# Column-group products of five places in a hybrid trunk issued as unbroken runs on TensorE

## The chip, the cores and the metric

One core of a Trainium2 chip runs the whole program in one launch. The metric is device time in microseconds (us), the median of three runs. The core has five engines that run side by side, each through its own list of instructions, in order: TensorE (PE in the profile; PEld is its weight load), VectorE (DVE), ScalarE (ACT), GpSimd (POOL) and SyncE (SP, which here only issues loads). They wait for each other at semaphores.

A matrix product on TensorE writes up to 128 partitions of PSUM. A *column-group product* has a stationary operand of only 32 or 64 columns and writes 32 or 64 partitions; four products of 32 columns, or two of 64, fill the width of the array.

## What is computed

Four layers over 256 latent and 256 context tokens of width 1024, each with another mixer and then a mixture of 16 experts (top 1 group of 4, top 2 experts in it). All in fp32.

```python
for i in range(DEPTH):                       # 4 layers
    mod_x = silu(c) @ w_mod[i] + b_mod[i]    # (1, 6*D); the same for the context, from c_ctx
    sh1, sc1, g1, sh2, sc2, g2 = split(mod, 6)
    h = rmsnorm(x) * (1 + sc1) + sh1
    y = [windowed_gqa, mamba2_bidir, mlstm_bidir, mla][i](h_ctx, h_lat, ...)
    x = x + g1 * y
    x = x + g2 * hier_moe(rmsnorm(x) * (1 + sc2) + sh2, ...)
return rmsnorm(x)
```

The five places of the change are the two rows `silu(c) @ w_mod`, the last product of each attention (`p @ v` in `windowed_gqa` and in `mla`), the product of `mamba2_bidir` inside a chunk (`einsum('blsg,blsge,bsgep->blgep', cb, lmat, u)`), and the chunk states of `mlstm_bidir` (`einsum('bsh,bshd,bshv->bhdv', ws, k, v)`).

## The kernel before

The program is written in Python and fully unrolled: 9,431 instructions on TensorE in the main part. A scheduler puts them in order. It walks the instructions with a priority (the order in which they are written) and with its own estimate of when operands are ready, and appends to each engine's list what is ready by that estimate; `issue_after(x)` adds "not before x on this engine", and `high_priority()` lets what is traced inside go ahead of other ready work. A product that is ready early by the estimate can thus be listed ahead of the products that belong beside it, with other work between them.

- **Modulation** (`mod_round`, product on L231). Each layer needs three rounds of 2048 columns. A round is 8 steps; a step loads a 1 MB piece of `w_mod` into a ring of four buffers `w` (`wload`, L182, on SP's queue, shared with the other weights) and makes four products, 32 columns stationary (`cs`, all steps), 512 wide, into the four quarters of one PSUM tile `wm`. 96 steps in all. Steps are put into a queue and popped by `fill` between pieces of the mixers, so they stand among the mixer's own products.
- **Values of layer 0** (`values`, L1128). For each of 4 token tiles and 4 key-value heads: transposes of the probabilities (L1118) into `tr`, ACT moves them to `PT` (L1122), then 4 or 8 products of 64 columns, 256 wide, into the two halves of a PSUM tile `core`, over `k` (2 or 4 key blocks) and `par` (even and odd heads). `probs` of the next block (scores, L1088) is written ahead of it.
- **Last product of a head pair in layer 1** (`head`, L1398): 8 products of 64 columns, 128 wide, for 16 pairs. It takes `A`, which DVE finished last.
- **mLSTM states** (`mlstm_states`, L1635): 12 times four products of 64 columns, 130 wide.
- **Values of layer 3** (`mla_core`, L1927): 8 times 8 products of 64 columns, 256 wide, over 4 key blocks and `h` (two heads).

The large plain products around them come from `mm3` (L207 to L209): a product of split fp32 as three passes.

Of the kernel before, what the change touches and what calls it, by code (L numbers as in the profile page):

```python
# [23 lines left out]
class Trunk:  # L24
# [172 lines left out]
    def split(self, pool, w, shape, name="split", bufs=3):  # L197
# [5 lines left out]
        return hi, lo  # L203

    def mm3(self, ps, a, b, start, stop):
        mm = self.nc.tensor.matmul
        mm(ps, a[0], b[0], start=start, stop=False)  # L207
        mm(ps, a[0], b[1], start=False, stop=False)  # L208
        self.last_mm = mm(ps, a[1], b[0], start=False, stop=stop)  # L209


    def mod_round(self, i, r):

        nc, I = self.nc, self.I
        st = {}

        def step(j, load=None):
# [11 lines left out]
            w = load([src]) if load else self.wload(src, [128, 2048])  # L229
            for g in range(4):  # L230
                nc.tensor.matmul(st["ps"][32 * g:32 * g + 32, :], self.cs[:, j, :], w[:, 512 * g:512 * g + 512],  # L231
                                 start=(j == 0), stop=(j == 7))

# [828 lines left out]
    def attn_core(self, pool, pout, kz, vr, qT):  # L1062
# [45 lines left out]
        def values(t, kv, pr, sm):  # L1108
# [16 lines left out]
            po = self.core()  # L1125
            for k in range(nk):
                for par in range(2):
                    nc.tensor.matmul(po[par * 64:(par + 1) * 64, :256], vr[:, k, kv * 64:(kv + 1) * 64],  # L1128
                                     PT[k // 2][:, k % 2, par::2, :], start=(k == 0), stop=(k == nk - 1))
            pv = po[:, :256].rearrange("p (m q) -> p m q", m=2)  # L1130
# [164 lines left out]
    def ssm_main(self, pool, late, mid, keep, heads):  # L1295
# [46 lines left out]
        def head(ft, zt, xs, xr, CT, Br, CB, gs, first):  # L1342
# [52 lines left out]
            py = self.core()  # L1395
            for c in range(4):
                for h in range(2):
                    nc.tensor.matmul(py[64 * h:64 * h + 64, tok(c)], xr[:, 128 * c + 64 * h:128 * c + 64 * h + 64],  # L1398
                                     M[0][:, h, c, :], start=True, stop=True)
            y = xs  # L1400
# [208 lines left out]
    def mlstm_states(self, pool, keep, kT, va, gt):  # L1609
# [16 lines left out]
        for d, order in ((0, (0, 1, 2, 3)), (1, (1, 0, 3, 2))):  # L1626
            for n in range(3):
                c, nx = order[n], order[n + 1]
                s = keep.tile([128, 4, 130], F32, name=f"cst{d}{n}")
                for ab in range(2):  # L1630
                    ps = self.core()
                    for a in (2 * ab, 2 * ab + 1):
                        for h in range(2):
                            hd = 2 * a + h
                            nc.tensor.matmul(ps[64 * h:64 * h + 64, (a % 2) * 130:(a % 2) * 130 + 130],  # L1635
                                             kw[c, d][:, hd * 64:hd * 64 + 64], va[c][:, hd, :], start=True, stop=True)
                    for a in (2 * ab, 2 * ab + 1):
                        v = ps[:, (a % 2) * 130:(a % 2) * 130 + 130]
                        if n == 0:
                            nc.scalar.activation(s[:, a, :], v, AF.Copy)  # L1640
                        else:
                            nc.vector.scalar_tensor_tensor(s[:, a, :], st[c, d][:, a, :], gt["cw"][:, d, a, c:c + 1], v,
                                                           op0=OP.mult, op1=OP.add)
                st[nx, d] = s
# [249 lines left out]
    def mla_core(self, pool, kT, vr, qT, ohi, olo):  # L1894
        nc, I = self.nc, self.I
        sc = 96.0 ** -0.5
        for a in range(8):
            po = self.core()
            PT = []
            for h in range(2):  # L1900
# [22 lines left out]
                PT.append(pt)  # L1923
            for k in range(4):
                for h in range(2):
                    hd = 2 * a + h
                    nc.tensor.matmul(po[64 * h:64 * h + 64, :256], vr[k][:, hd * 64:hd * 64 + 64],  # L1927
                                     PT[h][:, k].rearrange("p t q -> p (t q)"), start=(k == 0), stop=(k == 3))
            hh, ll = ohi[a // 2][:, a % 2, :], olo[a // 2][:, a % 2, :]
# [154 lines left out]
```

## Time and profile before

| | |
|---|---|
| runs | 2065.24 us median (2065.15 to 2068.01) |
| profiled execution | 2062.44 us, of which the span of instructions is 2060.3 us |
| TensorE busy | 1899.6 us (92%) |
| VectorE busy | 1394.9 us (68%) |
| ScalarE busy | 1036.1 us (50%) |
| GpSimd busy | 536.4 us (26%) |
| granted TensorE clock, mean | 0.963 of 2.4 GHz |
| read from memory | 452.41 MB, 234 GB/s over the span with what is written |

In the rows of a timeline, the first number is the start in us from the begin of the span, the second how long it lasted, then engine, line, operation, what it writes and reads, shape (partitions times columns of the stationary operand, then the moving operand), count. An fp32 product leaves two records in the trace, so "x8" of L231 is four products. Products are pipelined: how long one holds TensorE is read from its start to the start of the next instruction, not from its own length.

### The profile page before, as it was taken

How to read it: one execution, taken by the hardware profiler on the slowest of the kernel's cores; microseconds unless marked ns; L12 is line 12 of the kernel's file. 1: busy time of each engine (PE TensorE's matmuls, PEld its weight loads, DVE VectorE, ACT ScalarE, POOL GpSimd, SP SyncE). 2: the span in 40 equal slices, each digit the busy share in tenths (PEclk: the TensorE clock that was granted, in tenths of full speed). 3: DMA queues.
4: the chain of work that ended last, by engine and by line, in shares of the span. 5: the costliest groups of instructions: out<-in, count | busy, mean ns of one | idle time of the engine just before them, and what ended most of it. 6: DMA issues, size and time to landing. Idle time of an engine off the chain costs nothing. (4 is left out here: it accounts for less than half of the span.)

```text
span 2060.3 us, 30756 instructions
## 1 busy us (share of the span) xinstructions
PE 1899.6 (92%) x11036; PEld 1411.8 (69%) x11036; DVE 1394.9 (68%) x2728; ACT 1036.1 (50%) x2172; POOL 536.4 (26%) x525
## 2 busy tenths in 40 slices
PE   5999988999999999998799899996979999998996
PEld 2875686777767778776577678885867766656542
DVE  3568557886598787777788662338578876486444
ACT  2447526775575555433577542245457755454111
POOL 2012232213475555445221410004241132001000
PEclk8999998999999999999899999998989999999998
DMA  9344667986486546547798557542669966807792
GB/s 342 137 164 166 244 208 275 400 304 191 135 252 210 158 169 200 180 141 269 266 391 339 164 163 265 189 164 90 236 215 378 401 194 228 296 11 277 285 368 94
DMA packets 172915, 471.73 MB, mean 229 GB/s; under 512 B 27769, under 2 KB 74993, under 8 KB 152272
## 3 DMA queue, kind: packets, MB, share of 16 engines
q1 hardware_dynamic: 148912, 401.98, 54.3%
q0 software_dynamic: 23136, 65.86, 10.0%
q8 instruction: 90, 1.47, 0.3%
q10 hardware_dynamic: 704, 1.82, 0.2%
q14 instruction: 73, 0.60, 0.1%
HBM read 452.41 MB, written 29.77 MB: 234 GB/s over the span
## 5 line engine op out<-in xcount | busy, mean ns | idle before, releaser
L758 DVE TENSOR_TENSOR elo<-wl,ehi 128x1024 fp32r<-128x1024 f32 x156 | 187.0, 1220 | 27.8 <-ACT ehi L757 26.9
L757 ACT ACTIVATE ehi<-wl 128x1024 fp32r<-128x1024 f32 x156 | 161.6, 1055 | 51.8 <-PE acc L209 32.7
L231 PE MATMUL wm<-w,cs 128*32 128x512 f32 x768 | 125.2, 640 | 22.7 <-DMA w<-in_w_mod_dram 22.7
L763 POOL DMA_INDIRECT xg<-hd,gi x48 | 64.0, 1334 | 281.9 <-PE tr L776 224.0
L1292 POOL TENSOR_TENSOR wcl<-w,wch 128x512 fp32r<-128x512 f32 x76 | 114.2, 1515 | 81.8 <-ACT wch L1291 75.7
L207 PE MATMUL acc<-hhi,wch 128*128 128x512 f32 (+1 forms) x336 | 131.8, 393 | 0.5 <-ACT wch L1291 0.5
L209 PE MATMUL acc<-split_hi,hlo 128*128 128x256 f32 x464 | 131.3, 285 | 0.0
L209 PE MATMUL acc<-hhi,wcl 128*128 128x512 f32 (+1 forms) x336 | 129.8, 388 | 1.4 <-POOL wcl L1292 1.4
L208 PE MATMUL acc<-split_lo,hhi 128*128 128x256 f32 x464 | 131.0, 285 | 0.0
L207 PE MATMUL acc<-split_hi,hhi 128*128 128x256 f32 x464 | 131.0, 286 | 0.0
L208 PE MATMUL acc<-hlo,wch 128*128 128x512 f32 (+1 forms) x336 | 129.9, 387 | 0.0
L207 PE MATMUL acc<-ehi,xTh 128*128 128x512 f32 x288 | 123.6, 429 | 2.2 <-ACT xTh L779 2.2
L208 PE MATMUL acc<-elo,xTh 128*128 128x512 f32 x288 | 117.8, 409 | 1.1 <-DVE elo L758 1.1
L209 PE MATMUL acc<-ehi,xTl 128*128 128x512 f32 x288 | 115.6, 401 | 0.0
L758 DVE TENSOR_TENSOR elo<-w,ehi 128x1024 fp32r<-128x1024 f32 x84 | 100.9, 1218 | 13.6 <-ACT ehi L757 13.1
L757 ACT ACTIVATE ehi<-w 128x1024 fp32r<-128x1024 f32 x84 | 87.0, 1052 | 26.2 <-PE acc L209 14.8
L1370 ACT ACTIVATE A<-A,lnb 128x128 f32<-128x128 f32 x256 | 78.6, 388 | 39.4 <-POOL A L1365 39.4
L207 PEld LDWEIGHTS acc<-split_hi,hhi 128*128 128x128 f32 x464 | 88.1, 191 | 9.4 <-issue 3.5
L202 DVE TENSOR_TENSOR split_lo<-w,split_hi 128x1024 fp32r<-128x1024 f32 x33 | 40.1, 1224 | 80.3 <-ACT split_hi L201 80.0
L209 PEld LDWEIGHTS acc<-split_hi,hlo 128*128 128x128 f32 x464 | 88.5, 191 | 3.2 <-DVE split_lo L202 0.8
L386 POOL TENSOR_TENSOR x<-x,restmp 128x256 f32<-128x256 f32 (+1 forms) x46 | 48.2, 1047 | 160.1 <-DVE restmp L382 146.0
L208 PEld LDWEIGHTS acc<-split_lo,hhi 128*128 128x128 f32 x464 | 88.5, 191 | 0.7 <-issue 0.7
(625 smaller groups left out, 5456.9 us busy)
## 6 DMA issues: line engine op xcount, KB each, us to landing
w<-in_w_mod_dram SPq DMA_DIRECT2D x96, 1024.0 KB
wl<-in_moe_w_down_dram SPq DMA_DIRECT2D x47, 1024.0 KB
wl<-in_moe_w_gate_dram SPq DMA_DIRECT2D x82, 512.0 KB
wl<-in_moe_w_up_dram SPq DMA_DIRECT2D x82, 512.0 KB
w<-in_moe_w_gate_dram SPq DMA_DIRECT2D x46, 512.0 KB
w<-in_moe_w_up_dram SPq DMA_DIRECT2D x46, 512.0 KB
w<-in_ssm_w_in_dram SPq DMA_DIRECT2D x40, 512.0 KB
yd<-y POOLq DMA_DIRECT2D x39, 512.0 KB, 9.6
```

The lines of the kernel that those rows point to most:

```text
L202: self.nc.vector.tensor_sub(lo, w, hi)
L207: mm(ps, a[0], b[0], start=start, stop=False)
L208: mm(ps, a[0], b[1], start=False, stop=False)
L209: self.last_mm = mm(ps, a[1], b[0], start=False, stop=stop)
L231: nc.tensor.matmul(st["ps"][32 * g:32 * g + 32, :], self.cs[:, j, :], w[:, 512 * g:512 * g + 512], start=(j == 0), stop=(j == 7))
L386: (nc.vector if last else nc.gpsimd).tensor_add(x, x, tmp)
L757: nc.scalar.activation(hi, v, AF.Copy)
L758: nc.vector.tensor_sub(lo, v, hi)
L763: nc.gpsimd.indirect_dma_start(out=xgs[e % len(xgs)], out_offset=None, in_=self.hd, in_offset=bass.IndirectOffsetOnAxis(ap=self.gi[:, e:e ...
L1292: (eng or self.nc.gpsimd).tensor_sub(lo, v, hi)
L1370: nc.scalar.activation(M[d][:, h, c], M[d][:, h, c], AF.Exp, bias=self.lb[:, c, k:k + 1])
```

## The change

A helper `together` issues the products of a group so that all but the first get high priority and an edge behind the first. Five loops use it. Two of them also go in another order: in layer 0 the values start with the last key block and the odd heads, in layer 3 with the second head of the pair. No product, load or copy is added or taken away.

```diff
+    def together(self, jobs):
+
+        jobs = list(jobs)
+        first = jobs[0]()
+        with self.tc.issue_after(first.ins), self.tc.high_priority():
+            for m in jobs[1:]:
+                m()
+
...
-            for g in range(4):
-                nc.tensor.matmul(st["ps"][32 * g:32 * g + 32, :], self.cs[:, j, :], w[:, 512 * g:512 * g + 512],
-                                 start=(j == 0), stop=(j == 7))
+            self.together(lambda g=g: nc.tensor.matmul(
+                st["ps"][32 * g:32 * g + 32, :], self.cs[:, j, :], w[:, 512 * g:512 * g + 512],
+                start=(j == 0), stop=(j == 7)) for g in range(4))
...
-            for k in range(nk):
-                for par in range(2):
-                    nc.tensor.matmul(po[par * 64:(par + 1) * 64, :256], vr[:, k, kv * 64:(kv + 1) * 64],
-                                     PT[k // 2][:, k % 2, par::2, :], start=(k == 0), stop=(k == nk - 1))
+            self.together(lambda k=k, par=par: nc.tensor.matmul(
+                po[par * 64:(par + 1) * 64, :256], vr[:, k, kv * 64:(kv + 1) * 64],
+                PT[k // 2][:, k % 2, par::2, :], start=(k == nk - 1), stop=(k == 0))
+                for k in range(nk - 1, -1, -1) for par in (1, 0))
...
-            for c in range(4):
-                for h in range(2):
-                    nc.tensor.matmul(py[64 * h:64 * h + 64, tok(c)], xr[:, 128 * c + 64 * h:128 * c + 64 * h + 64],
-                                     M[0][:, h, c, :], start=True, stop=True)
+            self.together(lambda c=c, h=h: nc.tensor.matmul(
+                py[64 * h:64 * h + 64, tok(c)], xr[:, 128 * c + 64 * h:128 * c + 64 * h + 64],
+                M[0][:, h, c, :], start=True, stop=True) for c in range(4) for h in range(2))
```

The mLSTM states (order kept) and the values of layer 3 (`for k in range(4) for h in (1, 0)`) are rewritten in the same way.

What the scheduler makes of it, counted in TensorE's order. A run is an unbroken stretch of products of one place (two neighbouring steps make one run); in a run, each four products of 32 columns, or two of 64, are one started four or pair, and a rest counts as one.

| place | groups | broken before | runs before, after | fours or pairs before, after |
|---|---|---|---|---|
| modulation | 96 | 18 | 91, 74 | 115, 96 |
| values, layer 0 | 16 | 14 | 31, 16 | 62, 48 |
| last product, layer 1 | 16 | 9 | 30, 16 | 73, 64 |
| mLSTM states | 12 | 2 | 11, 11 | 26, 24 |
| values, layer 3 | 8 | 7 | 15, 8 | 39, 32 |

After the change no group is broken. The rest of the order is nearly kept: the lists hold the same instructions, and 2,690 of 9,431 on TensorE stand at another place, few of them by more than 30. Ten modulation steps begin 22 to 168 instructions earlier than before; no step's load moves by more than 4 places in SP's queue.

TensorE in layer 1, two modulation steps (`w_8217`, `w_8223`) among products of the output projection (`acc`) and of the heads' states (`core_7992`, `tr_7987`). Before; the other three products of `w_8223` stand 124 instructions further on:

```order
L1379 MATMUL core_7992<-ud_7951,Br_7399 128x128 x2
L231 MATMUL wm_7028<-w_8217,cs_78 32x512 x3
L1393 MATMUL tr_7987<-CT_7398,st0_7981 128x128
L231 MATMUL wm_7028<-w_8217,cs_78 32x512
L231 MATMUL wm_7028<-w_8223,cs_78 32x512
L207 MATMUL acc_7875<-wch_7859,yh0_7024 128x512
```

After:

```order
L1387 MATMUL core_7992<-ud_7951,Br_7399 128x128
L238 MATMUL wm_7028<-w_8217,cs_78 32x512 x4
L1401 MATMUL tr_7987<-CT_7398,st0_7981 128x128 x2
L238 MATMUL wm_7028<-w_8223,cs_78 32x512 x4
L215 MATMUL acc_7875<-wch_7859,yh0_7024 128x512
```

Both steps are whole; `w_8223` has come together at the place of its first product.

TensorE in layer 0, the value products `core_2277` of one block, with transposes `tr` of it and of the next block, and scores `acc` (each ended by a mask product on `identb`). Before:

```order
L1118 MATMUL tr_2270<-ident_85,p_2142 128x128 x4
L1128 MATMUL core_2277<-PT_2243,vr_214 64x256
L1118 MATMUL tr_2340<-ident_85,p_2210 128x128 x4
L1088 MATMUL acc_2391<-kh1_208,qT1_216 128x512
L1088 MATMUL acc_2391<-kl1_209,qT1_216 128x512
L1093 LDWEIGHTS identb_87
L1093 MATMUL acc_2391<-mj1_1354,identb_87 128x128
L1088 MATMUL acc_2400<-kh1_208,qT1_216 128x512
L1088 MATMUL acc_2400<-kl1_209,qT1_216 128x512
L1093 LDWEIGHTS identb_87
L1093 MATMUL acc_2400<-mj1_1354,identb_87 128x128
L1128 MATMUL core_2277<-PT_2243,vr_214 64x256 x3
```

After:

```order
L1126 MATMUL tr_2270<-ident_85,p_2142 128x128 x4
L1126 MATMUL tr_2340<-ident_85,p_2210 128x128 x4
L1134 MATMUL core_2277<-PT_2244,vr_214 64x256 x4
L1134 MATMUL core_2277<-PT_2243,vr_214 64x256 x4
L1126 MATMUL tr_2348<-ident_85,p_2219 128x128 x4
```

The lone product is gone, and the run begins with the operand that is made last (`PT_2244`, the second half of the key blocks); the scores that stood between the last transposes and the run stand elsewhere.

TensorE at the start of layer 3, two modulation steps (`w_17371`, `w_17377`) among the products of the latent projection (`acc_17162`, `acc_17205`). After the change they stand here:

```order
L217 MATMUL acc_17162<-lkv_hi_17152,hlo0_16944 128x288
L238 MATMUL wm_17352<-w_17371,cs_78 32x512 x4
L337 MATMUL tr_17031<-dg_17017,x1_70 128x128 x4
L337 MATMUL tr_17068<-dg_17066,x2_71 128x128 x4
L215 MATMUL acc_17162<-lkv_hi_17152,hhi1_16943 128x288
L216 MATMUL acc_17162<-lkv_lo_17153,hhi1_16943 128x288
L215 MATMUL acc_17205<-lkv_hi_17148,hhi0_16942 128x288
L216 MATMUL acc_17205<-lkv_lo_17149,hhi0_16942 128x288
L238 MATMUL wm_17352<-w_17377,cs_78 32x512 x4
```

Before, the first began 36 instructions later than here and the second 82 later, the first of them broken in two:

```order
L329 MATMUL tr_17080<-dg_17066,x2_71 128x128 x4
L231 MATMUL wm_17352<-w_17371,cs_78 32x512
L329 MATMUL tr_17116<-dg_17114,x3_72 128x128 x4
...
L208 MATMUL acc_17248<-lkv_lo_17153,hhi1_16943 128x288
L231 MATMUL wm_17352<-w_17371,cs_78 32x512 x3
L1813 MATMUL tr_17197<-ident_85,lrow_17189 128x128 x2
```

These are two of the ten steps that have moved ahead by more than 20 instructions.

## Rows read from the trace of the kernel before

**Rows 1.** The page, part 1: busy us of each engine (share), instructions.

```profile
PE 1899.6 (92%) x11036; PEld 1411.8 (69%) x11036; DVE 1394.9 (68%) x2728; ACT 1036.1 (50%) x2172; POOL 536.4 (26%) x525
```

**Rows 2.** Windows: length, then PE, PEld, DVE, ACT, POOL busy, clock, DMA, GB/s.

```profile
40.00:131.00 91.00, 90.64 (x729) 81.07 (x730) 54.63 (x126) 38.92 (x86) 0.58 (x1) 1.00 0.45 163
135.00:245.00 110.00, 106.31 (x672) 59.29 (x671) 78.34 (x253) 75.49 (x256) 30.92 (x29) 0.96 0.52 183
545.00:945.00 400.00, 392.60 (x2135) 300.39 (x2133) 314.50 (x506) 208.60 (x504) 206.79 (x153) 1.00 0.59 189
...
1705.00:1795.00 90.00, 82.08 (x525) 57.75 (x526) 49.85 (x98) 44.11 (x105) 8.39 (x14) 0.94 0.70 249
1805.00:1866.00 61.00, 60.51 (x314) 32.88 (x312) 50.14 (x146) 33.47 (x85) 0.00 (x0) 1.00 0.12 38
```

**Rows 3.** Lines by form: count, busy us, mean ns, idle us before, what ended it.

```profile
L231 PE MATMUL wm<-w,cs 128*32 128x512 f32 x768 | 125.2, 640 | 22.7 <-DMA w<-in_w_mod_dram 22.7
...
L1128 PE MATMUL core<-PT,vr 128*64 128x256 f32 x192 | 33.7, 392 | 0.5 <-ACT PT L1122 0.5
...
L1398 PE MATMUL core<-A,xr 128*64 128x128 f32 x256 | 22.9, 287 | 0.0
```

**Rows 4.** Timeline of PE in layer 0's projection: a whole and a lone L231.

```profile
42.85 1.07 PE L231 MATMUL wm<-w,cs 128*32 128x512 f32 x8
43.85 0.39 PE L209 MATMUL acc<-split_hi,hlo 128*128 128x256 f32 x1
...
50.97 0.28 PE L207 MATMUL acc<-split_hi,hhi 128*128 128x256 f32 x1
51.09 0.28 PE L208 MATMUL acc<-split_lo,hhi 128*128 128x256 f32 x1
51.30 1.04 PE L231 MATMUL wm<-w,cs 128*32 128x512 f32 x2
52.28 0.38 PE L209 MATMUL acc<-split_hi,hlo 128*128 128x256 f32 x1
52.50 0.28 PE L207 MATMUL acc<-split_hi,hhi 128*128 128x256 f32 x1
```

**Rows 5.** Timeline of PE in layer 0's attention: a broken value group.

```profile
231.10 0.66 PE L1118 MATMUL tr<-ident,p 128*128 128x128 f32 x4
231.69 0.65 PE L1128 MATMUL core<-PT,vr 128*64 128x256 f32 x2
232.27 0.66 PE L1118 MATMUL tr<-ident,p 128*128 128x128 f32 x4
232.85 1.94 PE L1128 MATMUL core<-PT,vr 128*64 128x256 f32 x14
234.72 1.09 PE L1118 MATMUL tr<-ident,p 128*128 128x128 f32 x8
```

**Rows 6.** Timeline of PE in layer 1: a whole and a broken last product.

```profile
578.42 1.09 PE L1398 MATMUL core<-A,xr 128*64 128x128 f32 x16
579.44 0.49 PE L1379 MATMUL core<-ud,Br 128*128 128x128 f32 x2
...
663.67 0.49 PE L1393 MATMUL tr<-CT,st 128*128 128x128 f32 x2
664.09 0.44 PE L1398 MATMUL core<-A,xr 128*64 128x128 f32 x4
664.46 0.71 PE L1393 MATMUL tr<-CT,st 128*128 128x128 f32 x4
```

**Rows 7.** Timeline of PE and ACT in layer 0: last transposes and their move.

```profile
236.18 0.63 PE L1118 MATMUL tr<-ident,p 128*128 128x128 f32 x4 [0.36 <-issue]
...
236.84 0.66 ACT L1122 ACTIVATE PT<-tr 128x256 f32<-128x256 f32 x2 [0.21 <-PE tr L1118]
```

**Rows 8.** Timeline of SP and PE in layer 2: a load and its products.

```profile
1437.09 0.33 SPq L182 DMA_DIRECT2D w<-in_w_mod_dram  x1
...
1442.03 1.07 PE L231 MATMUL wm<-w,cs 128*32 128x512 f32 x8 [0.81 <-DMA w<-in_w_mod_dram]
```

More of the change, by code (lines that the diff above doesn't have):

```diff
@@ L1631, in mlstm_states @@
                     ps = self.core()
[L1632 to L1636, printed above, removed]
+                    self.together(lambda a=a, h=h: nc.tensor.matmul(
+                        ps[64 * h:64 * h + 64, (a % 2) * 130:(a % 2) * 130 + 130],
+                        kw[c, d][:, (2 * a + h) * 64:(2 * a + h) * 64 + 64], va[c][:, 2 * a + h, :],
+                        start=True, stop=True) for a in (2 * ab, 2 * ab + 1) for h in range(2))
                     for a in (2 * ab, 2 * ab + 1):
@@ L1923, in mla_core @@
                 PT.append(pt)
[L1924 to L1928, printed above, removed]
+            self.together(lambda k=k, h=h: nc.tensor.matmul(
+                po[64 * h:64 * h + 64, :256], vr[k][:, (2 * a + h) * 64:(2 * a + h) * 64 + 64],
+                PT[h][:, k].rearrange("p t q -> p (t q)"), start=(k == 0), stop=(k == 3))
+                for k in range(4) for h in (1, 0))
             hh, ll = ohi[a // 2][:, a % 2, :], olo[a // 2][:, a % 2, :]
```

## Prediction

> **What bounds the kernel now.** I read the page's busy line first: TensorE is busy 92% of the span, VectorE 68%, ScalarE 50% [rows 1]. That is a mean, so the table of windows came next, for the stretches in which the five places stand [rows 2]. Compare PE with DVE in each. In layer 0's projection PE is busy 90.64 of 91 us, DVE 54.63. In layer 0's attention PE has 106.31 of 110, DVE 78.34, ACT 75.49. In layer 1's mixer PE has 392.60 of 400, DVE 314.50 (79%). At layer 3's start PE has 82.08 of 90, with the most transfers (DMA share 0.70). In layer 3's attention PE has 60.51 of 61 and DVE 50.14. So PE sets the pace in all of them, with nothing much in reserve on DVE in layer 1 and in both attentions. The groups by line say what ends PE's idle time [rows 3]: ahead of the values 0.5 us in all, ahead of layer 1's last products none, ahead of the modulation 22.7 us, all of it by the load of `w`. A us that one of these products holds PE for nothing is a us of the end, except where another engine is just behind.
>
> The timeline then gives the price of a broken group, from starts to next starts. A whole modulation step, four products, holds PE from 42.85 to 43.85, 1.00 us; a lone product of the same shape holds it from 51.30 to 52.28, 0.98 us [rows 4]. The four quarters run side by side, and a product cut off from its three neighbours pays for all of them.
>
> **The change part by part.** It neither adds nor removes an instruction; it saves fours and pairs, and the two ends of each run.
>
> *Price of a four, a pair and an end.* A product split off costs a further four. A lone four costs 0.98; I take 0.86 for one more inside a neighbouring run and 0.12 as fixed, since a usual step between plain products of this stage is 0.12 (50.97 to 51.09). The ends: 51.09 to 51.30 is 0.21 where 0.12 is usual, and 52.28 to 52.50 is 0.22 where 0.12 is usual, so 0.19 for both ends together [rows 4]. A run less thus saves 0.31 beside its fours. Values, 256 wide: a lone product takes 231.69 to 232.27, 0.58 us; seven (four pairs) take 232.85 to 234.72, 1.87 [rows 5]. The difference, 1.29 for three pairs, is 0.43 a pair, and 0.15 of the lone one is fixed; with the 0.19 a run costs 0.34. Layer 1's last products: eight take 578.42 to 579.44, 1.02, and a two-product piece 664.09 to 664.46, 0.37 [rows 6]; the difference over three pairs is 0.22 a pair, fixed again 0.15.
>
> *The sum.* Counts are those of the table under the change. Modulation: 19 fours by 0.86 and 17 runs by 0.31, 21.6 us. Values of layer 0: 14 pairs by 0.43 and 15 runs by 0.34, 11.1. Layer 1's last products: 9 by 0.22 and 14 by 0.34, 6.7. mLSTM states: 2 pairs by about 0.22 (130 wide, nearest to 128), 0.4. Values of layer 3: no row of theirs stands here; they have the shape of layer 0's, so 7 by 0.43 and 7 by 0.34, 5.4, with bounds from nothing to that. Together 45.2 us of PE's time. By stage, with the modulation's fours and runs counted in the order: layer 0 projection 2 fours and 1 run, 2.0; layer 0 attention 11.1; layer 1 mixer 11 and 10, 12.6, and 6.7, so 19.3; layer 2 mixer 3 and 3, 3.5, and 0.4, so 3.9; layer 3 start 3 and 3, 3.5; layer 3 attention 5.4.
>
> The Trainium skill (TensorE: Matmul & The Clock Gate, section "The mechanism" of Part 3) says the opposite of the row on which this rests: a weight load overlaps a running product only where the row group differs, and these four share all 128 rows and differ in columns alone. By that rule four would cost 4 times 0.98 instead of 1.00, an unbroken step would save nothing but the ends, and the kernel would stay where it is; by the row it saves as above, and the row decides.
>
> *What is late next, layer 0.* The run of values now starts with the operand that is made last (second place of the order). The last four transposes begin at 236.18 and ACT has moved them at 236.84 + 0.66 = 237.50, 1.32 us later [rows 7]. Before, scores stood between them and the rest of the values; now in places only one set of transposes does (231.10 to 231.69, 0.59 [rows 5]), and the head of the run would wait up to 0.73. Where nothing stands between, it waits about 1.3 less the transposes' own 0.6. The bounds are nothing and 1.32 for each of 16 blocks. I count 4 of 16 blocks, those at the end where no scores are left to go between, at 0.8: 3.2 lost, 7.9 left. Behind the waiting product everything on PE queues; transposes and scores of the next block then reach ACT and DVE later, but PE is what these wait for.
>
> *Layer 1.* DVE is busy 79% and the products that go into the run take `A`, its last product. I let 80% of 19.3 through, 15.4; bounds a quarter and all of it.
>
> *Layer 2* passes whole, 3.9. *Layer 3 start:* steps `w_17371` and `w_17377` have moved ahead by 36 and 82 instructions (third place of the order) while their loads stand where they stood in SP's queue. From a load's issue to its first product 4.94 us pass where PE is already waiting, and 0.81 of that was wait (1437.09 to 1442.03) [rows 8]. The bounds for a moved step are nothing (the ring holds four pieces, so a load is issued ahead) and 4.9; I let half of the 3.5 go, 1.7 left. *Layer 3 attention:* DVE 50.14 of 61 [rows 2]; 80% of 5.4, 4.3.
>
> Sum: 2.0 + 7.9 + 15.4 + 3.9 + 1.7 + 4.3 = 35.2 us. The profiled execution took 2062.4 (2060.3 span and 2.1 around it), so 2027.2; the median of the runs lies 2.8 above that execution, which gives 2030.
>
> **The rivals.** *A, forecast:* 2030, its own range 2020 (all 45.2 pass) to 2043 (half of it). *B, another engine takes over:* in layer 0's attention, layer 1 and layer 3's attention only a quarter comes through, (11.1 + 19.3 + 5.4)/4 = 9.0, with the other 7.6 makes 16.6, so 2049. For it: ACT and DVE above two thirds of layer 0's window, DVE 79 to 82% in the others. Against it: PE has next to no idle time there, so nothing else was ever the last to end [rows 2, 3].
>
> *C, the heads wait:* each of the 24 value runs (16 and 8) waits 1.32 for its last operand, 31.7; in place of the 3.2 above that leaves 6.7, so 2059. For it: the first product now takes the newest operand. Against it: the broken groups had a product right behind the newest operand too, and idled 0.5 us in all 192 [rows 3]. The same section of the Trainium skill says that products start and end strictly in order, by which a waiting head holds up all behind it; the 0.36 of idle time in [rows 7] is of that kind.
>
> *D, slower:* the ten modulation steps that begin 22 to 168 instructions earlier each wait for a whole load. Ten by 4.94 is 49.4, against 45.2 saved: 4.2 lost, 2069. It decides from a mean wait of 4.5 us. For it: a load's end is the one thing that ends idle time ahead of this line, 22.7 us already [rows 3]. Against: those are spread over 96 steps, and DMA has half its time free in layer 1 (share 0.59) [rows 2].
>
> *E, the change does nothing:* unbroken products don't run side by side after all, and a run of four costs four times 0.98: 2065. Against it stands the whole step of 1.00 us, and 78 of the 96 steps were whole already, so they give no other price than the one in [rows 4].
>
> **How the numbers follow.** A 0.64, B 0.21, C 0.06, D 0.06, E 0.03. The time is A's, 2030. The range goes from 2017, all of the 45.2 with prices 7% higher, to 2053, just above B; D, E and most of C lie outside it. A change of less than 0.2%, 4 us, can't be told from none here. Faster: A, B and half of C, 0.88. Same: the other half of C and E, 0.06. Slower: D, 0.06.
>
> **What would show it.** Of the profile after: every modulation record in the timeline comes as eight or a multiple, holding PE about 1.00 us for four (prices); the busy time of PE falls by 2 in layer 0's projection and some 19 over layer 1 (sums); the values of layer 0 show idle time ahead of them by ACT's `PT` of about 3 us, not 20 (A against C); the modulation's idle time by DMA stays near 22.7, at most a few us more (A against D); DVE's and ACT's share of the stages rises as these become shorter, with PE's idle share still small (A against B). I am wrong if PE's stages shrink but an idle share of the same size appears in them (B, C, D), or if single products of a column group turn out to be cheaper elsewhere than in the two places that I priced.

## The result and the profile after

The changed kernel takes 2029.79 us (median of 4 runs, 2027.54 to 2031.01), the kernel before 2065.19 in the same comparison (2064.59 to 2068.01): ratio 0.9829, 95% interval 0.9816 to 0.9842, or 35 us less. The forecast was 2030. The profiled execution took 2027.54, its span is 2025.7; of before these were 2062.44 and 2060.3.

The page of the changed kernel, part 1 (it answers to [rows 1]). TensorE is busy 39 us less and its weight loads (PEld) 14 less; the other engines work as long as before:

```profile
PE 1860.5 (92%) x11036; PEld 1398.2 (69%) x11036; DVE 1393.5 (69%) x2728; ACT 1035.9 (51%) x2172; POOL 535.5 (26%) x525
```

Groups by line and form, of after (answering to [rows 3]; the last is layer 3's values). The busy time of the modulation falls from 125.2 to 107.0, of layer 0's values from 33.7 to 24.3, of layer 1's last products from 22.9 to 17.5, of layer 3's values from 20.7 (first line, of before) to 15.6:

```profile
L1927 PE MATMUL core<-PT,vr 128*64 128x256 f32 x128 | 20.7, 389 | 0.2 <-ACT PT L1920 0.2
...
L238 PE MATMUL wm<-w,cs 128*32 128x512 f32 x768 | 107.0, 645 | 22.3 <-DMA w<-in_w_mod_dram 22.3
...
L1134 PE MATMUL core<-PT,vr 128*64 128x256 f32 x192 | 24.3, 388 | 1.8 <-ACT PT L1130 1.7
L1404 PE MATMUL core<-A,xr 128*64 128x128 f32 x256 | 17.5, 279 | 0.0
L1930 PE MATMUL core<-PT,vr 128*64 128x256 f32 x128 | 15.6, 385 | 0.7 <-ACT PT L1926 0.7
```

Two places in TensorE's timeline of after. The modulation step that was broken in [rows 4] has come together (51.27 to 52.26, 0.99 us, where one product alone had taken 0.98); and the value products of layer 0 come as 16 records, eight products, in 1.88 us, with a short wait for their last operand:

```profile
51.27 1.07 PE L238 MATMUL wm<-w,cs 128*32 128x512 f32 x8
52.26 0.38 PE L217 MATMUL acc<-split_hi,hlo 128*128 128x256 f32 x1
...
219.94 1.04 PE L1126 MATMUL tr<-ident,p 128*128 128x128 f32 x8
221.29 1.95 PE L1134 MATMUL core<-PT,vr 128*64 128x256 f32 x16 [0.31 <-ACT PT L1130]
223.17 1.09 PE L1126 MATMUL tr<-ident,p 128*128 128x128 f32 x8
```

Where the time came from is read from windows that begin and end with the same instructions in both kernels: layer 0's projection, layer 0's attention, layer 1's mixer, layer 1's experts with the norm behind them, layer 2's projections and states, layer 2's chunks with the output projection, layer 3's start, layer 3's attention. Columns as in [rows 2]. Of before:

```profile
40.94:129.90 88.96, 88.62 (x716) 79.05 (x714) 52.61 (x120) 37.98 (x85) 0.58 (x1) 1.00 0.44 161
129.90:245.88 115.98, 108.77 (x690) 61.12 (x686) 83.69 (x268) 78.74 (x262) 30.92 (x29) 0.96 0.52 183
506.13:965.35 459.22, 449.56 (x2461) 346.87 (x2461) 349.76 (x559) 234.11 (x548) 230.22 (x172) 0.99 0.59 191
965.35:1184.37 219.02, 195.80 (x957) 146.78 (x956) 178.25 (x300) 139.04 (x221) 59.38 (x68) 0.95 0.79 284
1184.37:1372.01 187.64, 186.64 (x1363) 154.41 (x1362) 68.05 (x138) 59.09 (x111) 11.94 (x22) 1.00 0.56 197
1372.01:1501.00 128.99, 104.56 (x759) 94.38 (x760) 93.50 (x255) 66.82 (x203) 43.34 (x43) 0.92 0.44 156
1712.15:1801.54 89.39, 82.02 (x528) 60.10 (x527) 47.38 (x90) 43.40 (x104) 9.18 (x15) 0.94 0.71 254
1801.54:1867.11 65.57, 64.02 (x323) 34.13 (x321) 52.93 (x153) 36.22 (x91) 0.86 (x2) 1.00 0.15 52
```

The same of after:

```profile
40.92:127.88 86.96, 86.62 (x715) 78.66 (x714) 52.62 (x120) 38.28 (x85) 0.58 (x1) 1.00 0.47 165
127.88:236.49 108.61, 99.31 (x691) 57.61 (x687) 83.50 (x268) 77.61 (x262) 31.02 (x29) 0.97 0.52 179
495.97:940.36 444.39, 432.74 (x2461) 342.46 (x2460) 352.11 (x562) 234.88 (x549) 225.35 (x173) 0.99 0.60 198
940.36:1162.75 222.39, 198.61 (x958) 148.94 (x956) 176.90 (x298) 138.86 (x221) 60.26 (x67) 0.93 0.78 280
1162.75:1347.89 185.14, 184.09 (x1364) 153.73 (x1362) 68.40 (x138) 59.35 (x111) 11.99 (x22) 1.00 0.57 200
1347.89:1470.52 122.63, 102.51 (x763) 92.50 (x764) 92.25 (x256) 67.05 (x203) 43.70 (x43) 0.93 0.46 164
1683.03:1770.59 87.56, 78.26 (x519) 59.42 (x518) 46.52 (x90) 42.59 (x102) 10.33 (x16) 0.92 0.71 259
1770.59:1832.48 61.89, 59.26 (x323) 33.19 (x321) 52.06 (x153) 36.20 (x91) 0.00 (x0) 1.00 0.15 53
```

Length less PE busy is TensorE's idle time. Against the forecast (left forecast, right measured, us; layer 2 is its two windows together):

| stage | PE busy less | idle more | stage shorter |
|---|---|---|---|
| layer 0 projection | 2.0, 2.0 | 0, 0 | 2.0, 2.0 |
| layer 0 attention | 11.1, 9.5 | 3.2, 2.1 | 7.9, 7.4 |
| layer 1 mixer | 19.3, 16.8 | 3.9, 2.0 | 15.4, 14.8 |
| layer 2 mixer | 3.9, 4.6 | 0, -4.3 | 3.9, 8.9 |
| layer 3 start | 3.5, 3.8 | 1.8, 1.9 | 1.7, 1.8 |
| layer 3 attention | 5.4, 4.8 | 1.1, 1.1 | 4.3, 3.7 |
| sum | 45.2, 41.5 | 10.0, 2.8 | 35.2, 38.6 |

The spans differ by 34.6, so the rest of the program became 4.0 longer, most of it layer 1's experts (219.02 to 222.39). One row of the table isn't what it seems. Of the moved modulation steps one left layer 3's start for the stretch ahead of it, so the windows of layer 3's start don't hold the same work: 112 records of the modulation before and 104 after, eight less, which is one step of four products. In these windows of L231 and L238 alone PE's busy time stands behind the length:

```profile
1712.15:1801.54 89.39, 17.62 (x112) 0.94 0.71 254
1683.03:1770.59 87.56, 13.64 (x104) 0.92 0.71 259
```

With a step at 1.0 us, layer 3's start saved 2.8 of PE's time and became 0.8 shorter, and 1.0 of the 4.0 elsewhere is that step. Four of six stages came out within 0.6 us of the forecast and layer 3's start 0.9 below it; layer 2 gave 5 us more, and the rest of the program took 3 back.

### The profile page after: what moved, and what is told of

The parts are those of the page before. It is cut to its first block, busy times and chain, and to the rows that moved or that the text cites. A ratio compares the mean times of both kernels' runs of the same rounds, so it can differ in the third digit from the quotient of the medians.

```text
span 2025.7 us, 30765 instructions
## 1 busy us (share of the span) xinstructions
PE 1860.5 (92%) x11036; PEld 1398.2 (69%) x11036; DVE 1393.5 (69%) x2728; ACT 1035.9 (51%) x2172; POOL 535.5 (26%) x525
## 5 line engine op out<-in xcount | busy, mean ns | idle before, releaser
L238 PE MATMUL wm<-w,cs 128*32 128x512 f32 x768 | 107.0, 645 | 22.3 <-DMA w<-in_w_mod_dram 22.3
```

Source lines behind the costliest of these rows:

```text
L238: self.together(lambda g=g: nc.tensor.matmul(st["ps"][32 * g:32 * g + 32, :], self.cs[:, j, :], w[:, 512 * g:512 * g + 512], start=(j == 0 ...
```

## The experiments

**Each place by itself.** Five kernels take one hunk of the change each and leave the other places as before. Of the modulation:

```diff
-            for g in range(4):
-                nc.tensor.matmul(st["ps"][32 * g:32 * g + 32, :], self.cs[:, j, :], ...
+            self.together(lambda g=g: nc.tensor.matmul(
+                st["ps"][32 * g:32 * g + 32, :], self.cs[:, j, :], ...
```

> Only the modulation steps are made unbroken. In TensorE's order their runs go from 91 to 74 and their fours from 115 to 96, as in the full change; the other four places stay broken (values of layer 0 31 runs, last products 29, values of layer 3 15). Theory (prices of fours and ends, each passed on as in the stages of the prediction): 2.0 + 12.6 by 0.8 + 3.5 + 1.7 = 17 us less than before, 2048. Rival (the gain of the full change came from the rest of the order, which the scheduler also changed): the loss per place can't be added up, and this kernel lies outside 2043 to 2053. In layer 2's last chunk the scores stand in TensorE's order as one block of 8, not in two of 4 as after the full change; if that order is what took 4 us of idle time out of layer 2's mixer, the idle time there stays near 24 us here.

Of layer 0's values:

```diff
-            for k in range(nk):
-                for par in range(2):
+            self.together(lambda k=k, par=par: ...
+                for k in range(nk - 1, -1, -1) for par in (1, 0))
```

> Only the values of layer 0 are made unbroken (31 runs to 16, 62 pairs to 48), and with them the scheduler happens to save 2 runs and 1 four of the modulation. Theory: 11.1 us of TensorE's time, of which some 2 to 3 come back as idle time in the attention; 8 to 9 less, and 1 for the modulation: about 2056. Rival (waits at the heads of the 16 runs, up to 1.3 us each): 2062 or more, with idle time ahead of the values well above the 1.8 us of the full change.

Of layer 1's last products:

```diff
-            for c in range(4):
-                for h in range(2):
+            self.together(lambda c=c, h=h: ... for c in range(4) for h in range(2))
```

> Only layer 1's last products are made unbroken (30 runs to 16, 73 pairs to 64); the modulation loses 3 runs and 1 four by the way. Theory of prices alone: 6.7 and 1.8 us by 0.8, so 7 less: 2058. In layer 2's last chunk TensorE's order is here the same as after the full change (the scores in two blocks of 4), though nothing in layer 2 was changed. If that order is what took the idle time out of layer 2's mixer, a further 4 us go there, idle time 20 us in place of 24, and the time is 2054. If the idle time went for another reason (the modulation steps or the states), it stays at 24 and the time is 2058.

Of layer 3's values:

```diff
-            for k in range(4):
-                for h in range(2):
+            self.together(lambda k=k, h=h: ... for k in range(4) for h in (1, 0))
```

> Only the values of layer 3 are made unbroken (15 runs to 8, 39 pairs to 32); all else stands as before. Theory: 5.4 us of TensorE's time less in layer 3's attention, about 1 of it back as idle time: 4 less, 2061, and no other stage changes by more than 1. Rival (DVE takes over there): 1.4 less, 2064, with the freed time as idle time ended by DVE.

Of layer 2's states:

```diff
-                    for a in (2 * ab, 2 * ab + 1):
-                        for h in range(2):
+                    self.together(lambda a=a, h=h: ... for a in (2 * ab, 2 * ab + 1) for h in range(2))
```

> Only the states of layer 2 are made unbroken (26 pairs to 24, runs 11 as before). Theory: 0.4 us, which can't be told from none: 2065 within 3 us, and the idle time of layer 2's mixer stays near 24 us. If the states were what took it out, it is 20 here and the time 2061.

| kernel | median, us | ratio to before (95%) | own stages shorter by, us | layer 2 chunks and output, us |
|---|---|---|---|---|
| modulation | 2040.55 | 0.9875 (0.9857 to 0.9893) | 2.0, 7.9, 2.4, 2.0 | 120.25 |
| values, layer 0 | 2049.80 | 0.9915 (0.9900 to 0.9929) | 6.6 | 120.70 |
| last products, layer 1 | 2058.02 | 0.9959 (0.9943 to 0.9975) | 5.4 | 122.70 |
| values, layer 3 | 2060.73 | 0.9974 (0.9964 to 0.9983) | 3.7 | 128.87 |
| states, layer 2 | 2062.89 (one run) | | | 128.82 |
| before | 2066.18 (2065.34 beside the states) | | | 128.99 |

In its own stages each place gives about what it gives in the full change: in layer 1's mixer 7.9 and 5.4 alone, 14.8 together; in layer 0's attention 6.6 and 7.4; in layer 3's 3.7 and 3.7. So the part that comes from the prices adds up. (The last 2.0 of the modulation is layer 3's start, from which the same step has moved out as in the full change.)

Modulation alone was forecast at 2048, and a time outside 2043 to 2053 was to show that the losses can't be added up. It came out below: its layer 1 gave 7.9 where 10.1 stood in the sum, but layer 2's chunks gave 8.7. Values of layer 0, forecast at 2056, came out 6 below that. They and the last products change nothing in layer 2, and gave 8.3 and 6.3 in the same window. That part can't be added up: any one of the three brings it. The last products have a median of 2058, as the prices alone say, although the idle time in layer 2's chunks went from 24.4 to 21.3, for which 2054 was forecast. (Their profiled execution took 2052.09, 6 below their median, so their windows come from a quick one.) Values of layer 3 and the states came out as forecast, 2061 and 2065 within 3; but with the values of layer 3 alone other stages moved by more than the 1 us allowed for, layer 1's experts by 1.7 up and layer 3's start by 1.5 down. So much a stage can differ between two kernels with next to the same order in it.

Idle time ahead of layer 0's values is 1.8 us with these alone too, so the heads of the runs hardly wait.

**The price of a break.** A product of zeros over the whole width of the array is put behind each modulation step, or into its middle:

```diff
+            jobs = [... the four products ...]
+            if i + r > 0 and 1 <= j <= 6:
+                jobs.insert(4, lambda: nc.tensor.matmul(
+                    st["ps"][:, :2], self.zw, w[:, :2], start=False, stop=False))
+            self.together(jobs)
```

> The changed kernel, and in 66 modulation steps (six of each round but the first) a fifth product right behind the four: a stationary tile of zeros over the whole array (128 columns), 2 columns moving, added to the same tile, so nothing of the result changes. This is the measure for the next kernel: its modulation has 96 fours still, in 89 runs instead of 74. Expected 5 us for the 15 ends (0.31 each) and 66 times 0.1 to 0.2 for the products: 10 to 20 us above the changed kernel.

In the second kernel it is `jobs.insert(2, ...)`.

> The same 66 products of zeros, but between the second and the third product of a step in place of behind the fourth. The modulation then has 154 fours started instead of 96, in 145 runs instead of 89; nothing else differs. Theory (products of different column groups run side by side only when they follow each other): 58 by 0.86 and 56 by 0.31 make 67 us more than with the product behind, less what idle time hides, so 55 to 67. Rival (a break costs only its ends, and the parts run as fast apart as together): 56 by 0.19, 11 us. By the Trainium skill's page on TensorE, section The mechanism, weight loads overlap running products only in another row group; the products of a step share theirs, so that a break there would cost the ends alone.

2039.42 and 2096.92 us, one run each: 57.5 us for the place of the product, where 55 to 67 was expected and 11 by the rival. The first also came out near its expectation (9.6 above the changed kernel, a little less than 10 to 20). TensorE's timeline, with the product behind:

```profile
1219.87 1.06 PE L240 MATMUL wm<-w,cs 128*32 128x512 f32 x8
1220.86 0.38 PE L244 MATMUL wm<-w,zw 128*128 128x2 f32 x2
1221.11 0.48 PE L217 MATMUL acc<-hhi,split_hi 128*128 128x512 f32 x1
```

and with it in the middle:

```profile
1252.44 1.05 PE L240 MATMUL wm<-w,cs 128*32 128x512 f32 x4
1253.42 0.38 PE L244 MATMUL wm<-w,zw 128*128 128x2 f32 x2
1253.73 1.05 PE L240 MATMUL wm<-w,cs 128*32 128x512 f32 x4
1254.72 0.50 PE L217 MATMUL acc<-hhi,split_hi 128*128 128x512 f32 x1
```

Four products and the full one hold TensorE 1.24 us (1219.87 to 1221.11), or 2.28 (1252.44 to 1254.72) when two stand on either side: each half takes 0.98 or 0.99, as the whole does. A break thus costs 1.04 us; 58 of them make 60, of which 57.5 arrived. (Layer 1's experts, which hold none of the breaks, were 3.9 shorter in the second kernel, so a single run can't confirm the 60 to better than some 4 us.) The Trainium skill (TensorE: Matmul & The Clock Gate, section "The mechanism") lets a weight load overlap a running product only where the row group differs. The trace disagrees: the four products of a whole step share the row group, and their eight loads lie within 0.16 us, under the first product. In the kernel before, at the whole step of [rows 4]:

```profile
42.85 0.16 PEld L231 LDWEIGHTS wm<-w,cs 128*32 128x32 f32 x8
```

That four products would then take four times 0.98 us was the prediction's own inference from a sentence on weight loads.

**Neighbours in one column group.** All four products of a step go into the same 32 partitions, nearly in the same runs (76 for 74). Three quarters of the modulation row are left with their first step by this, which makes the result wrong and leaves the instructions as they are:

```diff
+            q = [0, 1, 2, 3] if i + r == 0 or j == 0 else [0] * 4
...
-                st["ps"][32 * g:32 * g + 32, :], self.cs[:, j, :], ...
+                st["ps"][32 * q[g]:32 * q[g] + 32, :], self.cs[:, j, :], ...
...
```

> The changed kernel, but in 77 modulation steps (all but the first of each round, and but the first round) all four products write the same 32 partitions, one upon the other: the same instructions in the same runs (76), with one column group for all four. The modulation values are wrong by this, which changes the data and not the instructions. Theory (it is the four column groups that let them run side by side; being neighbours isn't enough): 77 by three further products of 0.86 make 199 us more than the changed kernel, less what waits for loads hide, so 150 to 200. Rival (neighbours with the same moving shape are cheap whatever columns they use): no more than 10 us.

2213.38 us, 183.6 above the changed kernel (150 to 200 expected). The four now hold TensorE 3.55 us:

```profile
1320.68 3.62 PE L239 MATMUL wm<-w,cs 128*32 128x512 f32 x8
1324.23 0.50 PE L215 MATMUL acc<-hhi,split_hi 128*128 128x512 f32 x1
```

A further product in the same columns costs 0.85, in other columns next to nothing. 77 steps by 2.55 make 196, of which 183.6 arrived; that the other 12 fell into waits that were there anyway is only argued. Being neighbours isn't the reason; being neighbours in different columns is. The four also write the same place of PSUM here, which wasn't tried apart. Layer 1's last products speak against that as the cause: there the products of one column group write different places, and a further pair still costs 0.22 us [rows 6], as an estimate from 0.85 for four times the columns would have it (0.21).

**The old order of the values.**

```diff
-                for k in range(nk - 1, -1, -1) for par in (1, 0))
+                for k in range(nk) for par in range(2))
...
-                for k in range(4) for h in (1, 0))
+                for k in range(4) for h in range(2))
```

> The changed kernel with the values of layers 0 and 3 in the order of before (first key block and even head first), still issued through the helper. The scheduler then lets the first product go as soon as its operand is ready by its estimate, and the rest follow when theirs are: in TensorE's order the values are broken as before (31 runs and 62 pairs in layer 0, 15 and 39 in layer 3), while the other places are whole. Theory (only runs and pairs count): the 7.4 and 3.7 us that these two stages gained go again, 11 us above the changed kernel, 2041. Rival (the edge and the priority matter by themselves): with the first product held for its successors' sake, the stages' time differs from that of before by more than 2 us.

2045.17 us (0.9921, 0.9901 to 0.9940; six runs between 2039.71 and 2052.90), 15 above the changed kernel where 11 was expected. The profiled execution is the quickest of them, 2039.71, 12 above the profiled one of the changed kernel. Windows of layer 0's attention, layer 2's chunks and output, layer 3's attention:

```profile
126.31:242.03 115.72, 108.36 (x691) 60.35 (x687) 83.58 (x268) 78.58 (x262) 30.96 (x29) 0.97 0.52 183
1349.69:1476.23 126.54, 104.81 (x764) 95.20 (x764) 92.62 (x256) 66.80 (x203) 43.76 (x43) 0.92 0.45 159
1779.05:1844.62 65.57, 64.03 (x323) 34.13 (x321) 52.95 (x153) 36.21 (x91) 0.00 (x0) 1.00 0.14 47
```

Both attentions are as long as before the change (115.98 and 65.57): without the reversal the helper doesn't hold these groups together (31 and 15 runs, as before), since the first product is placed by its own operand and the rest by theirs. The 11 us expected are these two. Layer 2's chunks are 3.9 longer too (126.54 against 122.63), and the other stretches gave 2.5 of it back, which makes the 12; the rest of the 15 has no profile.

**Layer 2's window.** What differs there between the kernels is TensorE's order, in the third of its four chunks a little and in the last one most. From the last chunk's scores on, one letter a product (Q scores, S values with `SD`, C states with `cst`, M modulation; runs of M cut), with the window's length:

```
before, values 3, states  QQQQQQQQSSSSCCSSCCCCSSCCCCSSSSCCSSCCSSMMMMMMMMMMMCCM  129.0 128.9 128.8
behind_before             QQQQQQQQSSSSCCSSCCCCSSCCCCSSSSCCSSCCSSCCMMM           130.0
two_steps_late            QQQQQQQQSSSSCCSSCCCCSSCCCCSSSSCCSSCCSSCCMMM           133.3
old_order                 QQQQQQQQSSSSCCSSCCCCCCSSSSCCSSCCSSCCSSMMMMMMMMMMMMCCM 126.5
two_steps                 QQQQQQQQSSSSCCSSCCCCSSCCSSCCSSCCCCSSSSMMMMMMMMMMMMMMMMCCM 124.9
after, last products 1    QQQQSSQQQQSSCCCCCCSSCCSSCSSCSSCCSSCCCCSSMMM           122.6 122.7
modulation, values 0      QQQQQQQQSSSSCCSSCCCCCCSSCCSSSSCCCCSSCSSCMMM           120.3 120.7
```

Kernels that share a line have the same length within 0.5 us, whichever place they change, with two exceptions; the lines lie up to 13 us apart. `behind_before` and `two_steps_late` agree as far as the letters go and differ by 3.3: the second has one modulation step more in its window, and waits 1.2 us longer for the loads of `w`. The kernels with products of zeros, not in the list, have the letters of `old_order` but for these products, and took 123.9 (behind) and 125.4 (in the middle) where `old_order` took 126.5.

The first two chunks take the same time in all, within 0.1 us. The last one, from its scores to the modulation behind it, took 20.5 us before, 16.3 after and 13.9 with the modulation alone, and the granted clock of that stretch isn't the same:

```profile
1415.44:1435.97 20.53, 14.48 (x77) 13.68 (x77) 17.88 (x42) 6.40 (x23) 8.13 (x7) 0.69 0.18 67
1388.17:1404.51 16.34, 11.87 (x83) 10.72 (x81) 16.34 (x45) 9.63 (x32) 7.27 (x6) 0.90 0.35 128
1404.40:1418.28 13.88, 11.32 (x82) 9.91 (x81) 13.88 (x44) 7.26 (x24) 6.78 (x6) 0.98 0.40 152
```

Its eight scores, one block before and with the modulation alone, show what the clock makes of them; before, TensorE had just stood for 2.91 us, and the clock granted over the 3.79 us was 0.50, the lower of its two levels (1.2 GHz):

```profile
1415.44 3.79 PE L1684 MATMUL core<-qz,kT 128*128 128x128 f32 x16 [2.91 <-ACT inter L1710]
1404.40 2.28 PE L1692 MATMUL core<-qz,kT 128*128 128x128 f32 x16
```

So of the 6.4 us that the change took out of the window, 4.2 lie in the last chunk, 2.6 of them PE's busy time, at a clock of 0.90 in place of 0.69, and 1.6 idle time; 3.1 lie in the third chunk (where two kernels with the order of before are 1.6 and 1.8 longer than it), and the output projection gave 1.0 back. With the modulation alone 6.7 of the 8.7 lie in the last chunk.

`behind_before` is the kernel before with one edge moved (the filled steps wait for `behind`), so that only the last pair of C comes ahead of M:

```diff
-                            nc.tensor.matmul(pi[:, d * 130:d * 130 + 130], qz[:, hd, :], ...
+                            behind = nc.tensor.matmul(pi[:, d * 130:d * 130 + 130], qz[:, hd, :], ...
```

> The kernel before, with one edge changed: in layer 2 the modulation steps that are filled in behind the last chunk must stand behind the chunk's last product with the states (cst), in place of behind its last product with the values. In TensorE's order the pair of cst products that stood behind 11 modulation products now stands ahead of all 20; the scores (core from qz and kT) stay one block of 8, as before. Nothing else moves by more than a few places. Open is what took 6 us out of layer 2's mixer (from the first scores to the end of the output projection) in kernels that changed nothing there. If it is the modulation products ahead of the last pair, that stretch goes from 129.0 to 123 us and the time to some 6 us less than before. If the split of the last scores into two blocks of 4 did it, the stretch stays at 126 or more: only the 2.7 us by which the pair comes earlier can be had, and the kernel is 3 us or less below before.

2063.45 us (0.9992, 0.9979 to 1.0005), window 130.0, no gain:

```profile
1374.46:1504.45 129.99, 106.34 (x763) 96.60 (x764) 93.65 (x256) 66.89 (x203) 43.46 (x43) 0.89 0.43 155
```

So the 6 us aren't the modulation ahead of the last pair. (The clock was lower here, 0.89 to 0.92, and PE busy 1.8 longer, so a small gain could be hidden; 6 us could not.) Nor is it the scores in two blocks of four: the shortest windows (120.25 and 120.70) have them in one block of eight, which speaks against the guess on record for `last1_only`. The order goes with the length of the window in most of these kernels, and the change altered it by the way. Which neighbours in it cost the time, and whether the order brings the lower clock through its waits or the clock comes by itself, stays open.

**Two steps in one run**, to save more ends:

```diff
+            if two:
+                a, b = part(j), part(j + 1)
+                self.together(a() + b())
...
-        return [lambda load=None, j=j: step(j, load) for j in range(8)] + [fin]
+        if i + r == 0:
+            return [lambda load=None, j=j: step(j, load) for j in range(8)] + [fin]
+        return [x for j in range(0, 8, 2) for x in (None, lambda j=j: step(j, two=True))] + [fin]
```

> The changed kernel with two modulation steps in one: both loads are issued, and then the eight products go as one unbroken run, at the place of the second step. Runs of the modulation go from 74 to 60, fours stay at 96. Theory: 14 ends by 0.31, 4.3 us less than the changed kernel, 2025. Rival (the load of the second step comes just ahead of its products, and two of the four buffers are asked for at once): idle time ahead of the modulation goes from 22 us to well above it, and the time is 2035 or more.

2029.31 us (0.9834, 0.9819 to 0.9848), where 2025 was expected: no difference from the changed kernel. Layer 1's mixer and layer 2's projections are 2 us shorter each (of the second, 1 is a step that now stands in layer 2's chunks), but layer 0's attention is 3.4 longer, with more waits for ACT's `p`, the probabilities. Layer 2's experts are 5.9 longer in the profiled execution, which is the slowest of the five (2034.18). (Modulation waits for loads 23.0 us, so the rival was not the reason.) Hence a last kernel without pairs in layer 0, and with the moved edge of `behind_before`:

```diff
-        if i + r == 0:
+        if i == 0 or (i, r) == (1, 0):
```

> The changed kernel with two modulation steps in one run, but only for the rounds that are filled in behind layer 0 (two steps in one cost 3 us there), and with the edge of the other kernel of this pair in layer 2. Runs of the modulation 67 (74 in the changed kernel). Theory: what two steps in one saved stage by stage, 2 us in layer 1's mixer, 2 in layer 2's projection and 2 at layer 3's start, without what it lost in layer 0: 2024 to 2026, better than both kernels. Rival (loads in twos come back as waits in layer 2's experts): 2030, no gain.

2035.08 us (0.9857, 0.9834 to 0.9880), where 2024 to 2026 was expected: 5 above the changed kernel, though the two intervals overlap. Layer 0's attention is mended (108.96), and layer 2's window has gone to 133.26, 10.6 longer, in the order of `behind_before`. Layer 2's experts are 4.5 longer, but with 4.2 more of PE's busy time at a clock of 0.94 in place of 0.97, so not by the waits for loads that the rival named. No version beat the changed kernel.

## Why the prediction was right, step by step

*A four costs as much as one product, and what the prediction counted is fours and ends.* Shown by the three kernels on the price: halves of 0.98 and 0.99 us, 0.85 for each further product in the same columns, 57.5 us for 58 breaks. Rival E is out. (That the saving is nothing else is not so: layer 2, below.)

*The size of the ends was too high.* A break was priced at 0.86 and 0.31, 1.17 together, and measured 1.04 between a full product and the halves. In the table the forecast 45.2 us of PE's time became 41.5, the shortfall where most runs were saved (layer 1, layer 0's attention). The two fixed terms, 0.12 and 0.19, are what was mis-sized: less 0.86 for the four, 0.18 is left around the zeros where 0.31 stood. In the places themselves an estimate from the table gives little more. Take the fours and pairs at their prices out of PE's saving, and 3.4 us over 15 runs are left in layer 0's attention, 5.4 over 24 in layer 1 and 1.8 over 7 in layer 3's attention: 0.22 to 0.25 a run, where 0.31 and 0.34 were forecast.

*Pass-through of the values.* Idle time in layer 0's attention rose by 2.1, against 3.2 forecast; ahead of the values themselves it is 1.8 us in 16 runs, 0.31 in the run shown above, not 1.32 each. Rivals B and C are out: both attentions and layer 1's mixer passed on over three quarters of PE's saving (7.4 of 9.5, 3.7 of 4.8, 14.8 of 16.8), and, as the rows above read, the eight transposes ahead of the run cover most of ACT's move: from their start at 219.94 to the run's 1.35 us pass, of which 0.31 is idle. (The 0.36 us of [rows 7] that the prediction counts with the waiting heads stands there as `issue`: the row names nothing that it waited for.)

*Layer 1.* 14.8 against 15.4. Idle time ended by DVE appeared as forecast, at a place of its own: transposes of the conv output wait for DVE's `xs`, 4.4 us in two waits, where the same view of before lists none for `xs`. The view of waits, PE, layer 1's mixer, after:

```profile
PE tr L1340 <- DVE xs L1278: 4.4, 2, 2.9
PE acc L215 <- ACT yh L1420: 2.8, 1, 2.8
PE tr L1401 <- DVE st L1394: 1.4, 2, 1.2
```

*Layer 3's start: the wrong reason, and a number that only looks right.* 1.7 us were forecast, the window became 1.8 shorter, and 1.0 of that is the step that moved out of it. Half of 3.5 us was given up to loads that would come late. The modulation waits for DMA as long as before (22.3 us, 22.7 before), and within this stage 0.7 against 0.6, so rival D is out and that step failed. What took the 1.9 us is, as the trace reads (it was not tried by itself), lost cover. Before, two modulation steps stood right ahead of the last transposes of `lrow`:

```profile
1743.25 1.92 PE L231 MATMUL wm<-w,cs 128*32 128x512 f32 x16
1745.10 0.57 PE L1813 MATMUL tr<-ident,lrow 128*128 128x128 f32 x3
```

After, they have gone ahead, and TensorE stands for 2.26 us until DVE has made `lrow`:

```profile
1713.33 0.44 PE L1819 MATMUL tr<-ident,lrow 128*128 128x128 f32 x2 [0.28 <-ACT lrowT L1822]
1716.03 0.66 PE L1819 MATMUL tr<-ident,lrow 128*128 128x128 f32 x2 [2.26 <-DVE lrow L1816]
```

*Layer 2, and the rest.* Passing whole was forecast; 5 us more came out of chunks whose own products the change doesn't touch, which goes with their order and their clock, and 4.0 went in the rest of the program, the moved step with it. The two nearly cancel. The mechanism and four stages were right; that the total came out to within 1 us is luck.

## What to carry to other kernels

Where a stationary operand is narrow, price a product by the unbroken run it stands in and not by its own length: one product with the columns to itself costs what four side by side cost. Look for groups that a scheduler has split, and issue the product with the latest operand first, since here no priority kept a group together whose head was ready before its tail. Then look at what the moved products used to cover, and at stretches that were put in another order by the way: here layer 2's chunks, in which little was to be had, moved by 6 us.

## What the runs showed of the hardware that was not expected

The same stretch, with the same instructions in nearly the same order, differs in length by up to 6 us from one kernel's profiled execution to another's, and its granted TensorE clock with it. Layer 1's experts and the norm behind them took 219.02 us at 0.95 before and 222.39 at 0.93 after; with the values of layer 0 alone 223.98 at 0.92, with two steps in one but late 217.63 at 0.95:

```profile
958.45:1182.43 223.98, 201.56 (x957) 150.49 (x956) 178.35 (x300) 139.16 (x221) 60.97 (x68) 0.92 0.77 278
```

```profile
939.85:1157.48 217.63, 195.89 (x957) 146.97 (x956) 176.22 (x298) 138.56 (x221) 60.19 (x67) 0.95 0.79 286
```

Of the 6.4 us between these two, PE's busy time makes 5.7 (201.56 and 195.89), so most of it is the same work at another mean between the clock's two levels, 1.2 and 2.4 GHz, and not a wait. Why the clock is lower in some of them was not tried, nor whether it differs as much between two executions of one kernel. Between before and after PE's busy time makes 2.8 of the 3.4, most of what the rest of the program took back.
